# One ScalarE pass of an add-and-GELU kernel, moved ahead of three copies

## The chip, the cores and the metric

The kernel runs on one core of a Trainium2 chip. The metric is the device time of one execution in microseconds (us). A core has several engines that run their own instruction streams side by side and wait for each other through semaphores: VectorE (DVE in the profile), ScalarE (ACT), GpSimd (POOL), SyncE (SP), which here only issues DMA transfers, and TensorE (PE), which this kernel does not use. Sixteen DMA engines move data between the chip's main memory (DRAM, or HBM in the profile) and the core's own memories.

## The reference

Two float32 matrices of 1024 x 4096 are added, and the tanh form of GELU is applied to each element:

```
def reference(x, y):
    z = x + y
    return (0.5 * z * (1 + np.tanh(np.sqrt(2 / np.pi) * (z + 0.044715 * z ** 3)))).astype(np.float32)
```

Each matrix has 16.78 MB; two are read and one is written, 50.33 MB in all.

## The kernel before

The 1024 rows are spread over 128 partitions, eight rows to each, so that a partition holds 32,768 elements. The kernel treats them as one line cut in two halves of 16,384. Tile `z` (line by line: x, then x + y, then the result) holds the whole line. Tile `y` holds only half a line, so y's second half can be loaded only when all adds of the first half have read y's first half. Tile `ps` is a buffer in PSUM, a second memory of the core, for copies of some of x's chunks.

Transfers are all issued by SP, in this order: y's first 704 columns and the rest of y's first half, x's first half, x's second half (four loads that wait for nothing), y's second half (waits for the adds of chunks 0 to 8), the first store (waits for the gelus of chunks 0 to 8), the second store (waits for the gelus of chunks 9 to 19). One function issues each kind: `load_x` (L130), `load_y` (L135), `store` (L139).

The work on the line is cut in 20 chunks. Chunks 0 and 1 have 1024 columns and chunks 2 to 8 have 2048; these are the first half. Chunk 9 has 512 columns, 10 has 1536, 11 to 16 have 2048, 17 has 1024, 18 and 19 have 512; these are the second half. For a chunk there are up to three steps:

- `copy(c)` (L143), on ScalarE, only for chunks 2 to 6 and 9 to 11: x's chunk is copied from `z` to `ps`.
- `add(c)` (L150): on VectorE, or for chunks 7, 8 and 12 on GpSimd. It reads x's chunk (from `ps` if there is a copy, else from `z`) and y's chunk, and writes the sum to `z`.
- `gelu(c)` (L162), on ScalarE: GELU of the chunk, in place in `z`.

The order on each engine is written out by hand in lists: `on_vector`, `on_gpsimd`, and for ScalarE `on_scalar` (L98), a list of steps and chunks. A loop at the end of the kernel takes the steps from these lists in turn and emits each once the steps that it needs have been emitted; the order within a list is never changed. ScalarE therefore does, in this order: copies 2 to 6, gelus 0 and 1, copies 9 to 11, gelus 2 to 19. Copies 9 to 11 need x's second half; gelu 2 needs only the add of chunk 2.

Two functions edit the finished program: one moves the first two loads ahead of the start-up barrier, the other lets the wait for the last store happen later. They are not touched.

Of the kernel before, what the change touches and what calls it, by code (L numbers as in the profile page):

```python
# [66 lines left out]
def kernel(  # L67
# [27 lines left out]
    copies = {2: 0, 3: 2048, 4: 0, 5: 2048, 6: 0, 9: 0, 10: 512, 11: 2048}  # L95
    on_vector = [0, 1, 2, 3, 4, 5, 6, 9, 10, 11, 13, 14, 15, 16, 17, 18, 19]
    on_gpsimd = [7, 8, 12]
    on_scalar = [("copy", c) for c in (2, 3, 4, 5, 6)] + [("gelu", 0), ("gelu", 1)] + [("copy", c) for c in (9, 10, 11)] + [("gelu", c) for c in range(2, 20)]  # L98
    held = {7: 1}

    def ranges(sizes):
# [137 lines left out]
```

## Time and profile before

| what | value |
|---|---|
| time, median of 3 runs (lowest to highest) | 120.17 us (120.0 to 120.55) |
| time of the profiled execution | 120.21 us |
| its span (first to last instruction or transfer in the profile) | 118.7 us |
| data moved, mean rate over the span | 50.33 MB, 424 GB/s |
| ScalarE busy | 44.1 us (37%), 30 instructions |
| VectorE busy | 29.1 us (25%), 18 instructions |
| GpSimd busy | 13.7 us (12%), 7 instructions |
| a gelu of 128 x 2048 | 1.90 us, 13 of them |
| a copy of 128 x 2048 | 1.87 us, 6 of them |
| an add of 128 x 2048 on VectorE / on GpSimd | 2.28 us / 4.53 us |

How the views are read: the order of time has, in each line, the start in us, the length, the engine, the line of the kernel (L162 is line 162), the operation, what it writes and reads (`z<-ps,y` writes z from ps and y), the shapes, how many instructions were merged (`x7`), and in brackets how long the engine had been idle before and what ended that. `SPq` is SP issuing a transfer; where two issues are merged (`x2`), the length reaches from the first to the end of the second. The chain that ended last is followed back from the end of the program, at each step to what released it. The view by stretches has, for each stretch of time, its length, the busy time of VectorE, ScalarE and GpSimd with the number of their instructions, the clock of TensorE (1.00 here, without meaning), the DMA engines' share and the GB/s moved. In this view a DMA packet is booked whole in the stretch in which it starts, so in a short stretch the share can exceed 1.

### The profile page before, as it was taken

The page shows a single profiled execution, that of the slowest core. Times are in us where ns is not written, and L with a number is a line of the kernel's source. Part 1 is how long each engine was busy: PE and PEld are TensorE (multiplying, and loading weights), DVE is VectorE, ACT ScalarE, POOL GpSimd, SP SyncE. Part 2 cuts the span into 40 slices and gives each one's busy share as a digit, 9 for nine tenths or more (in the row PEclk, how much of TensorE's full clock was granted, in tenths as well). Part 3 has the DMA queues.
Part 4 walks back from the last instruction along what each step waited for, and adds up shares of the span by engine and source line. Part 5 has one row for each costly group of instructions (what it writes and reads, how often), then busy time and mean ns, then how long its engine had stood idle before and what let it go on. Part 6 is the DMA issues. An engine that isn't in the chain of part 4 may idle for free.

```text
span 118.7 us, 115 instructions
## 1 busy us (share of the span) xinstructions
DVE 29.1 (25%) x18; ACT 44.1 (37%) x30; POOL 13.7 (12%) x7
## 2 busy tenths in 40 slices
DVE  0000000000000299992000000009999920000000
ACT  5000000000000296890069999804799980000000
POOL 0000000000000039960000000009500000000000
DMA  9779978988899889988898889988899888988891
GB/s 460 338 338 613 402 338 360 685 353 353 353 640 420 353 353 464 596 353 353 353 707 353 353 353 530 530 353 353 353 618 442 353 353 353 707 353 353 353 662 44
DMA packets 1008, 50.33 MB, mean 424 GB/s; under 512 B 112, under 2 KB 112, under 8 KB 240
## 3 DMA queue, kind: packets, MB, share of 16 engines
q1 hardware_dynamic: 1008, 50.33, 98.6%
HBM read 33.55 MB, written 16.78 MB: 424 GB/s over the span
## 4 chain that ended last, share of the span: by engine, by line
DMA 55%; DVE 14%; ACT 10%; DVEq 1%; ACTq 0%; issue 0%; SPq 0%
DMA z<-in_x_dram 33%; DMA y<-in_y_dram 22%; DVE z L150 14%; ACT z L162 10%; DVEq L206 1%; ACTq L206 0%; DVEq L150 0%; SPq L135 0%
## 5 line engine op out<-in xcount | busy, mean ns | idle before, releaser
L162 ACT ACTIVATE z<-z 128x2048 f32<-128x2048 f32 (+3 forms) x20 | 29.7, 1556 | 5.9 <-DVE z L150 5.9
L143 ACT COPY ps<-z 128x2048 f32<-128x2048 f32 (+2 forms) x8 | 13.0, 1654 | 46.3 <-DMA z<-in_x_dram 44.6
L150 DVE TENSOR_TENSOR z<-z,y 128x2048 f32<-128x2048 f32 (+2 forms) x9 | 13.6, 1573 | 39.5 <-DMA z<-in_x_dram 39.5
L150 DVE TENSOR_TENSOR z<-ps,y 128x2048 f32<-128x2048 f32 (+2 forms) x8 | 15.6, 2015 | 25.9 <-DMA y<-in_y_dram 25.9
L150 POOL TENSOR_TENSOR z<-z,y 128x2048 f32<-128x2048 f32 x3 | 13.5, 4526 | 70.7 <-DVE z L150 42.9
L191 ACT ACT_TABLE_LOAD x1 | 1.3, 1283 | 1.3 <-PEq L223 1.3
L190 DVE MEMSET one<- 128x1 f32 x1 | 0.1, 59 | 1.3 <-PEq L223 1.3
L191 ACT ACTIVATE one<-one 128x1 f32<-128x1 f32 x1 | 0.2, 202 | 0.0
L223 POOL MEMSET const-float32-0.0<- 128x1 f32 x1 | 0.1, 98 | 0.2 <-issue 0.2
L223 POOL MEMSET const-uint8-127<- 128x1 uint8 x1 | 0.1, 102 | 0.0
L223 POOL MEMSET const-bfloat16-1.0<- 128x1 bf16 x1 | 0.1, 101 | 0.0
L223 POOL MEMSET const-float32-1.0<- 128x1 f32 x1 | 0.1, 98 | 0.0
## 6 DMA issues: line engine op xcount, KB each, us to landing
y<-in_y_dram SPq DMA_DIRECT2D x1, 7840.0 KB, 21.0
y<-in_y_dram SPq DMA_DIRECT2D x1, 352.0 KB, 3.0
z<-in_x_dram SPq DMA_DIRECT2D x2, 49.0
out_dram<-z SPq DMA_DIRECT2D x2, 21.9
y<-in_y_dram SPq DMA_DIRECT2D x1, 25.7
```

Source lines behind the costliest of these rows:

```text
L143: nc.scalar.copy(out=in_psum(c), in_=zt[:, a:b])
L150: ins = eng.tensor_add(out=zt[:, a:b], in0=first, in1=yt[:, o : o + b - a])
L162: nc.scalar.activation(out=zt[:, a:b], in_=zt[:, a:b], func=act.Gelu_apprx_tanh)
L190: nc.vector.memset(one[:, :1], 0.0)
L191: nc.scalar.activation(out=one[:, :1], in_=one[:, :1], func=act.Gelu_apprx_tanh)
L206: tc.compile()
L223: nc = _bacc.Bacc("TRN2", target_bir_lowering=False, num_devices=1)
```

## The change

One list is edited. In ScalarE's order the gelu of chunk 2 stands behind gelu 1 and ahead of copies 9, 10 and 11; before, it stood behind these copies. No step is added or left out, and no size, buffer, engine or transfer changes.

```
-    on_scalar = [("copy", c) for c in (2, 3, 4, 5, 6)] + [("gelu", 0), ("gelu", 1)] + [("copy", c) for c in (9, 10, 11)] + [("gelu", c) for c in range(2, 20)]
+    on_scalar = [("copy", c) for c in (2, 3, 4, 5, 6)] + [("gelu", 0), ("gelu", 1), ("gelu", 2)] + [("copy", c) for c in (9, 10, 11)] + [("gelu", c) for c in range(3, 20)]
```

In the built program ScalarE's list differs in this alone: one gelu of 128 x 2048 stands ahead of the three copies, and six instead of seven stand behind them. The lists of VectorE, GpSimd and SP, and what each of their instructions waits for, are the same in both.

## The prediction

> **What bounds the kernel now.** I read the page first, for the share of the DMA engines, then the order of time, then the chain that ended last, and at last the DMA traffic in stretches of one microsecond.
>
> ```profile
> span 118.7 us, 115 instructions
> ...
> q1 hardware_dynamic: 1008, 50.33, 98.6%
> ```
>
> The one DMA queue keeps the 16 DMA engines at work for 98.6% of the span; ACT, the busiest compute engine, has 37%. So an ACT pass matters only through the moment at which it lets a transfer start. The order of time shows these moments:
>
> ```profile
> 51.72 2.00 ACT L162 ACTIVATE z<-z 128x1024 f32<-128x1024 f32 x2
> 54.35 0.33 SPq L135 DMA_DIRECT2D y<-in_y_dram  x1
> 60.28 3.76 ACT L143 COPY ps<-z 128x512 f32<-128x512 f32 x3 [6.56 <-DMA z<-in_x_dram]
> 63.98 12.70 ACT L162 ACTIVATE z<-z 128x2048 f32<-128x2048 f32 x7
> 76.70 21.29 SPq L139 DMA_DIRECT2D out_dram<-z  x2
> 80.14 4.55 DVE L150 TENSOR_TENSOR z<-ps,y 128x512 f32<-128x512 f32 x3 [25.86 <-DMA y<-in_y_dram]
> ...
> 84.72 12.89 ACT L162 ACTIVATE z<-z 128x2048 f32<-128x2048 f32 x9 [0.71 <-DVE z L150]
> ```
>
> ACT ends gelu 1 at 53.72 and stands still for 6.56 us until x's second half lands. Then come copies 9 to 11 and seven gelus (chunks 2 to 8), and at 76.70 SP issues the first store. But the second half of y, issued at 54.35, is still under way then: DVE gets it at 80.14. The issue of the first store is therefore not on the chain that ended last, which goes from y's second half straight to the second half's work:
>
> ```profile
> 54.35 25.67 DMA y<-in_y_dram
> ...
> 80.14 0.69 DVE z L150
> ...
> 84.72 11.86 ACT z L162 x7
> ...
> 97.10 0.52 ACT z L162
> ```
>
> The last view counts DMA packets by their start, in stretches of 1 us. A transfer of half a tensor is eight rounds of 16 packets of 64 KB, one per engine; a row with 1049 GB/s holds exactly one round (16 x 65,536 B in 1 us), and its DMA share (next to last column) is then the mean time of a packet in us.
>
> ```profile
> 54.50:55.50 1.00, 0.00 (x0) 0.00 (x0) 0.00 (x0) 1.00 2.43 1049
> 56.90:57.90 1.00, 0.00 (x0) 0.00 (x0) 0.00 (x0) 1.00 2.42 1049
> 59.30:60.30 1.00, 0.00 (x0) 0.02 (x1) 0.00 (x0) 1.00 2.43 1049
> 73.70:74.70 1.00, 0.00 (x0) 1.00 (x1) 0.00 (x0) 1.00 2.42 1049
> 76.10:77.10 1.00, 0.00 (x0) 0.57 (x1) 0.00 (x0) 1.00 2.66 1049
> 78.90:79.90 1.00, 0.00 (x0) 0.00 (x0) 0.00 (x0) 1.00 2.43 1049
> 95.80:96.80 1.00, 0.03 (x1) 1.00 (x2) 0.00 (x0) 1.00 2.42 1049
> 98.40:99.40 1.00, 0.00 (x0) 0.00 (x0) 0.00 (x0) 1.00 2.44 1049
> ```
>
> The rounds follow each other at the length of a packet, also from one transfer to the next: x's last round starts in 56.9 to 57.9 and y's first in 59.3 to 60.3. The reader is to see two things. First, y's last round (76.1 to 77.1) is followed by the first store's first round (78.9 to 79.9) with no hole: the store was there in time. Second, that last round alone took 2.66 us a packet, not 2.42. The store was issued in the midst of it (76.70).
>
> **The change, part by part.** *Moved out of the late run:* one gelu of 128x2048. Seven of them take 12.70 us, so one is 12.70 / 7 = 1.81 us (the mean of one, 1.90 us, overlaps its neighbour). Gelus 3 to 8 then run from 63.98 to 74.89, and the first store is issued at about 74.9 instead of 76.70.
>
> *Moved into the idle time:* gelu 2 runs from 53.72 to about 55.6. It issues no DMA. Its add ran third on DVE (two adds of 1024, then chunk 2, from 40.92 on) and ended near 45.5, so it waits for nothing. The copies behind it wait for x's second half until 60.28 as before: cost 0, hidden by 6.56 - 1.9 = 4.7 us of idle ACT; without that idle time it would be 1.81 us. On DVE 0.55 us of add 6 lie beside it (to 54.28); a lengthening there would delay the issue of y's second half, whose first packets start only after 59.3, so some 5 us cover that. DVE, GpSimd and SP keep their order and their waits. SP's queue has only the first store and, behind it, the second store, which waits for the last gelu (97.6) in both kernels.
>
> *The store's earlier issue.* The second store shows the lead that an issue needs: issued at 97.64, its first packets start in the row 98.40 to 99.40, so at most 1.76 us. The first store has 78.9 - 76.70 = 2.2 us at least. It was in time already, so 1.8 us more of lead fill no hole: 0 us from the wait itself. The queue has served transfers in the order of issue (y's first half, x's two halves and y's second half landed one after another), so y's second half should land at 80.0 as before, the second half's chain end at 97.6 and the span stay at 118.7.
>
> *The one price that the trace does not show* is what becomes of the slow last round. On the mean it loses 2.66 - 2.42 = 0.24 us. On the path it loses more: x's first half landed at 1.26 + 39.53 = 40.79, its second at about 1.6 + 58.6 = 60.2 (DMA issue to landing, longest), y's second half at 54.35 + 25.67 = 80.02; the steps are 19.4 and 19.8 us, so about 0.4 us. Three rows bound it. If it belongs to the change from loading to storing, it stays: 0. If it comes from the store's packets reaching the queue while the last load packets are in flight, an issue before that round starts (74.9, the round starts after 76.1) should cost what y's second half cost when it was issued at 54.35, ahead of x's last round: 2.43 and 2.42 us, that is 0.01; the gain is up to 0.4 us. If it grows with the time for which both are in the queue, it gets worse by 0.4 us (worked out below). I take 0: the round is the only one in which a load is followed by a store, and issues behind a load (54.35) and behind a store (97.64) cost 0.01 to 0.02 us a packet, so direction is the one thing that sets it apart beyond doubt.
>
> *Sum.* The profiled execution took 120.21 us, 118.7 of it span and 1.5 around it; it stands 0.04 above the median of 120.17. 120.21 + 0 (gelu 2 early) + 0 (store's wait) + 0 (slow round) = 120.2 us.
>
> **The rivals.**
>
> *A: the slow round goes.* The nearest row in position (issue one round ahead, 0.01 us) speaks for it, the different direction against it. Y's second half lands 0.4 us earlier, DVE and ACT follow, the second store is issued at 97.2 instead of 97.64, and the first store, whose packets are shifted by as much, ends in time for it. 120.21 - 0.4 = 119.8 us; with the slowest engine losing more than I read from the landings, down to 119.6.
>
> *B: the early store disturbs the load for longer.* Place: the last rounds of y's second half. An issue takes effect about 0.9 us later (97.64 to the first packets of the second store, taken as 98.5), so the store is in the queue from 77.6; y's last packets end about 79.7. That is 2.1 us for a loss of 0.4. Issued at 74.9 it would be there from 75.8, 3.9 us: 0.4 x 3.9 / 2.1 = 0.74, so 0.34 more. It passes to the end in full, because the second store has no slack: the first store's last round starts in 95.8 to 96.8 and ends 2.42 later, 98.2 to 99.2, just where the second store's packets begin. 120.21 + 0.34 = 120.55 us, slower than before. It decides from the moment at which the next to last round of y shows over 2.5 us a packet. Against it: the round of 73.70 and all before it are at 2.42 whatever ACT does, and an issue cost a load 0.01 where the next transfer was a load.
> The Trainium skill, "DMA: Bandwidth & Descriptors", section "Two DMAs through the same engine are not ordered", says that descriptors on one queue of an engine start in order but are pipelined, with reading and writing as separate queues. By that rule the store could begin to read while the load's last packets are still being written, which would speak for B; the trace shows a slow round there, but not what slows it.
>
> *C: load and store packets take turns.* If the store's packets, queued earlier, went ahead of y's last round, y would land a packet, 2.42 us, later, the last gelu would end at 100.0 and the second store start 2.42 us late: 120.21 + 2.4 = 122.6 us. Against it: no store packet started before y's last round in the trace, and queued transfers have landed in order.
>
> *D: the change does not do what it says*, because ACT's copies or the store wait for something else. The store would be issued at 76.7 again: 120.2 us. The listing of each engine's instructions speaks against it, the idle 6.56 us too; the time is the same as in the forecast.
>
> **How the numbers follow.** Forecast 0.53, A 0.30, B 0.10, C 0.03, D 0.02, something unseen 0.02. A measurement of this kernel tells about 0.5% (0.6 us) from no change: 119.57 and 120.77 are the bounds. A reaches past the lower one only if the slowest engine's loss is well above 0.4 us, a third of its chance: 0.10, and 0.02 for the unseen and the scatter of runs (120.0 to 120.55) on the forecast: faster 0.12. Slower: C 0.03, a third of B 0.03, scatter and unseen 0.03: 0.09. The rest, 0.79, is within 0.5%. The range reaches down to A's lowest, 119.6, and up past B to 120.7.
>
> **What would show it.** Gelu 2 at 53.7 and the copies still at 60.3; the first store issued at 74.9; its first packets still in 78.9 to 79.9, without a hole; DVE's first add of the second half at 80.1; the second store issued at 97.6. The row 76.10 to 77.10 decides between forecast (2.66), A (2.42) and B (over 2.66, and the row before it raised too). Store packets that start before 78 would be C. The prediction is wrong if y's second half lands more than 0.6 us earlier or later than 80.0, or if a hole opens between the two stores.

## The result and the profile after

The changed kernel is slower: 121.08 us in the median of 6 runs (120.82 to 121.48) against 120.19 for the kernel before (120.0 to 120.55), a ratio of 1.0081 with a 95% interval of 1.0064 to 1.0098. Its profiled execution took 120.98 us with a span of 119.5 us; before, these were 120.21 and 118.7.

The order of time, with the lines that answer to those shown of the kernel before:

```profile
51.75 3.80 ACT L162 ACTIVATE z<-z 128x1024 f32<-128x1024 f32 x3
54.38 0.33 SPq L135 DMA_DIRECT2D y<-in_y_dram  x1
60.32 3.76 ACT L143 COPY ps<-z 128x512 f32<-128x512 f32 x3 [4.77 <-DMA z<-in_x_dram]
64.02 10.90 ACT L162 ACTIVATE z<-z 128x2048 f32<-128x2048 f32 x6
74.94 23.86 SPq L139 DMA_DIRECT2D out_dram<-z  x2
80.95 4.55 DVE L150 TENSOR_TENSOR z<-ps,y 128x512 f32<-128x512 f32 x3 [26.64 <-DMA y<-in_y_dram]
...
85.54 12.89 ACT L162 ACTIVATE z<-z 128x2048 f32<-128x2048 f32 x9 [0.71 <-DVE z L150]
```

On ScalarE the change did what it says. Gelu 2 joined gelus 0 and 1 (x3, to 55.55), the copies began with x's second half as before, and the first store was issued at 74.94 instead of 76.70. But VectorE got y's second half at 80.95, not at 80.14. Everything behind it is late by the same 0.8 us: ScalarE's last run starts at 85.54 instead of 84.72. The chain that ended last names the piece that grew:

```profile
54.38 26.45 DMA y<-in_y_dram
...
80.95 0.69 DVE z L150
...
97.92 0.52 ACT z L162
```

y's second half took 26.45 us from issue to landing, 0.78 more than before (25.67). That is the whole growth of the span (119.5 - 118.7 = 0.8). The DMA packets by their start show where in that transfer it lies; as before, a row with 1049 GB/s holds one round of 16 packets of 64 KB, and its share is the mean time of a packet in us:

```profile
71.30:72.30 1.00, 0.00 (x0) 1.00 (x2) 0.00 (x0) 1.00 2.42 1049
73.70:74.70 1.00, 0.00 (x0) 1.00 (x1) 0.00 (x0) 1.00 2.43 1049
76.10:77.10 1.00, 0.00 (x0) 0.00 (x0) 0.00 (x0) 1.00 3.60 1049
79.70:80.70 1.00, 0.00 (x0) 0.00 (x0) 0.00 (x0) 1.00 2.43 1049
```

y's last round took 3.60 us a packet, where it had taken 2.66. The rounds before it, and the store's first round behind it (79.7 to 80.7), are at the usual 2.42 to 2.43. Issued 1.76 us earlier, the store did not start earlier: its first packets began at 79.9 us, where they had begun at 79.0. What changed is the one round ahead of it.

### The profile page after: what moved, and what is told of

Read it like the earlier page. It is cut to its first block, busy times and chain, and to the rows that moved or that the text cites. A ratio compares the mean times of both kernels' runs of the same rounds, so it can differ in the third digit from the quotient of the medians.

```text
span 119.5 us, 115 instructions
## 1 busy us (share of the span) xinstructions
DVE 29.1 (24%) x18; ACT 44.1 (37%) x30; POOL 13.8 (12%) x7
## 4 chain that ended last, share of the span: by engine, by line
DMA 55%; DVE 14%; ACT 10%; DVEq 1%; ACTq 0%; issue 0%; SPq 0%
DMA z<-in_x_dram 33%; DMA y<-in_y_dram 22%; DVE z L150 14%; ACT z L162 10%; DVEq L206 1%; ACTq L206 0%; DVEq L150 0%; SPq L135 0%
```

## The experiments

Theory 1: a store that stands in the queue behind y's second half slows y's last round. The first rivals are that gelu 2's new place costs the time in some other way, that every turn from load to store has a fixed price, and that the loss grows with the time in the queue (B of the prediction). The first four runs move the store's issue; later ones ask what of the store it is. For each, the loss is the share of y's last round less that of the round before it. It is read from two rows, 73.70 to 74.70 and 76.20 to 77.20 unless others are shown: in the kernel before 2.66 - 2.42 = 0.24 us, in the changed one 3.60 - 2.43 = 1.17. Each loss comes from one execution, and the rounds ahead of the last one lie between 2.42 and 2.48 us in these rows, so 0.05 us of a loss mean nothing.

Where the issue of the store is moved, a line from the order of time stands first: the store's issue, merged with that of the second store (x2).

**after_held: gelu 2 early, store late**

On the changed kernel, the end of ScalarE's list and the new step:

```
-[("gelu", c) for c in range(3, 20)]
+[("gelu", c) for c in range(3, 8)] + [("idle", 0), ("idle", 1)] + [("gelu", c) for c in range(8, 20)]
...
+    def idle(i):
+        a = 1024 * i
+        nc.scalar.activation(out=one[:, :992], in_=zt[:, a : a + 992], func=act.Gelu_apprx_tanh)
```

> Gelu 2 stays ahead of the copies, but ScalarE makes two more passes of 992 columns (of finished results, into a tile that nothing reads) ahead of gelu 8, so that the first store is issued near 76.8 us, where it was before the change, not at 74.9. Theory 1 (the early store in the queue slows y's last round): the round in 76.1 to 77.1 falls back from 3.60 to about 2.65 us a packet, and the time to 120.2 us. Rival (something else about gelu 2's new place costs the time, its pass in the idle stretch or the order of the copies): the time stays at 121.1 us.

```profile
77.06 20.85 SPq L139 DMA_DIRECT2D out_dram<-z  x2
...
73.70:74.70 1.00, 0.00 (x0) 0.97 (x2) 0.00 (x0) 1.00 2.46 1049
76.20:77.20 1.00, 0.00 (x0) 0.83 (x1) 0.00 (x0) 1.00 2.43 1049
```

With the store issued at 77.06, the loss was gone (2.43 after 2.46) and the time fell to 119.94 us, a ratio to the kernel before of 0.9992 (0.9971 to 1.0013). Gelu 2's new place by itself costs nothing that this interval shows: the first rival falls. The round came out faster than the 2.65 expected; the next run bears on that.

**g1_early: the store one more pass later than in the kernel before**

ScalarE's list behind copies 2 to 6, against the kernel before (for the next two runs as well):

```
-[("gelu", 0), ("gelu", 1)] + [("copy", c) for c in (9, 10, 11)] + [("gelu", c) for c in range(2, 20)]
+[("gelu", 0)] + [("copy", c) for c in (9, 10, 11)] + [("gelu", c) for c in range(1, 20)]
```

> Gelu 1 goes behind the copies too, so that the first store is issued about 0.95 us later than in the kernel before, at 77.65 us, and its packets can reach the queue from about 78.5 (second store before: 97.64 to 98.50). Theory 1: the last round of y is by then nearly done and takes 2.42 to 2.50 us a packet, y's second half lands at 79.6, no hole opens ahead of the store, and the time is 119.6 to 119.9 us. Rival (the slow round is the price of turning from loads to stores, whenever the store is issued): the round stays at 2.66 and the time at 120.2 us or a little above.

```profile
77.76 19.89 SPq L139 DMA_DIRECT2D out_dram<-z  x2
...
73.70:74.70 1.00, 0.00 (x0) 1.00 (x2) 0.00 (x0) 1.00 2.45 1049
76.20:77.20 1.00, 0.00 (x0) 1.00 (x1) 0.00 (x0) 1.00 2.44 1049
```

The store was issued at 77.76 and the loss was gone here too (2.44 after 2.45); the next packets followed without a hole. The time was 119.85 us, ratio 0.999 (0.9973 to 1.0006): in the expected direction, but not clear of 1. The same kernel was therefore run again, as **g1_again**:

> The same kernel as g1_early, for a narrower interval. Theory 1: 0.25 us of the slow round saved, 119.85 to 119.95 us, ratio 0.998. Rival: no difference, 1.000.

```profile
73.70:74.70 1.00, 0.00 (x0) 1.00 (x2) 0.00 (x0) 1.00 2.42 1049
76.20:77.20 1.00, 0.00 (x0) 1.00 (x1) 0.00 (x0) 1.00 2.43 1049
```

119.8 us against 120.16, ratio 0.9974 (0.9956 to 0.9992): this time clear of 1, by 0.26%, and the lowest median of all runs. The two series put the gain at 0.10% and 0.26%. In this chain y's second half took 25.20 us, 0.47 less than before. In both executions the turn from load to store cost nothing: it has no fixed price.

**g0_early: later still**

```
+[("copy", c) for c in (9, 10, 11)] + [("gelu", c) for c in range(0, 20)]
```

> Gelus 0 and 1 both go behind the copies: the first store is issued about 78.6 us, its packets can start from about 79.45. Theory 1: y's last round takes 2.42, y's second half lands at 79.6, but the engines stand still from about 79.0 until 79.45; the second store is then not waited for, and the span is about that of g1_early plus 0.3 us: 119.9 to 120.2 us. Rival (a price of turning): 2.66 and a hole of some tenths of a us on top: 120.6 us.

```profile
78.80 19.35 SPq L139 DMA_DIRECT2D out_dram<-z  x2
...
74.20:75.20 1.00, 0.00 (x0) 1.00 (x2) 0.00 (x0) 1.00 2.42 1049
76.70:77.70 1.00, 0.00 (x0) 1.00 (x2) 0.00 (x0) 1.00 2.42 1049
79.30:80.30 1.00, 0.01 (x1) 0.00 (x0) 0.00 (x0) 1.00 2.45 1049
```

The store was issued at 78.80. The last round is clean, but the store's first packets began 0.17 us after the first engine was free (79.65 against 79.48 in the trace). The time was 120.27 us, ratio 1.0023 (1.0008 to 1.0037), a little above the expected span. The hole is not all of it. In this execution seven of y's earlier rounds, from 55 to 72 us, took 2.47 to 2.52 us (2.42 to 2.43 in g1_again), so y's last packets ended at 79.48 to 79.81, over 0.5 us later than in g1_again, and the engine that was free last had no hole. Why these rounds were slow is not known. Without them the store, with its first packets at 79.65, would have been late on every engine (g1_again's ended their load at 78.83 to 79.29). So an issue at 78.80 is too late; of the moments tried, 77.06 and 77.75 cost nothing.

**g5_early: much earlier**

```
+[("gelu", c) for c in range(0, 5)] + [("copy", c) for c in (9, 10, 11)] + [("gelu", c) for c in range(5, 20)]
```

> Gelus 2, 3 and 4 all go into the idle stretch: the first store is issued about 71.3 us, two rounds of y ahead of its last one instead of just ahead of it. Theory 1 with a limit (only the last load packet can be slowed, by a store that is queued behind it): the last round takes 3.6 us as in the changed kernel, the rounds before it 2.42 to 2.43, and the time is 121.1 us as there. Rival B as it was predicted (the loss grows with the time for which both are in the queue): another 3.6 us in the queue, several rounds slow, 122 us or more.

```profile
71.49 27.39 SPq L139 DMA_DIRECT2D out_dram<-z  x2
...
73.70:74.70 1.00, 0.00 (x0) 0.00 (x0) 0.00 (x0) 1.00 2.46 1049
76.20:77.20 1.00, 0.00 (x0) 0.00 (x0) 0.00 (x0) 1.00 3.48 1049
```

Issued at 71.49, 3.45 us ahead of the changed kernel, the store cost no more: 3.48 - 2.46 = 1.02 us, and 121.08 us, the same median as the changed kernel (ratio to before 1.0088, 1.0069 to 1.0108). The loss has a limit and does not grow with the time in the queue. (The round ahead, 2.46, is above the 2.43 expected, but after_held shows the same 2.46 with no store in the queue.)

**s992 and s256: how many bytes stand behind the load.** Both are built on g1_early, whose last round is clean; the first new line is that of s992, the second that of s256.

```
-    stores = [16384, 16384]
+    stores = [992, 15392, 16384]
+    stores = [256, 16128, 16384]
```

> Built on g1_early. The first store is cut in two: 992 columns (31.7 KB per DMA engine, eight packets of 4 KB) are stored from 54.8 us on, queued right behind y's second half, the other 15,392 columns when gelu 8 is done, at 77.7. Theory H1 (behind the last load packet the engine already reads ahead for the store, and loses the time of what it reads, up to some 30 KB: 1.1 us at the 27 GB/s at which a 64 KB packet takes 2.42 us): y's last round takes about 3.4 us a packet, for 31.7 KB / 27.1 GB/s = 1.17 at most. Theory H2 (a price of about 1 us for each turn from load to store, whatever the store's size): 3.5 us as well. This run is the anchor for s256.

> As s992 with 256 columns (8.2 KB per engine, eight packets of 1 KB) in the early piece. H1: only 8.2 KB can be read ahead, 0.30 us, so y's last round takes about 2.7 us a packet. H2: about 3.5 us, as with the large store.

s992, then s256:

```profile
73.70:74.70 1.00, 0.00 (x0) 1.00 (x2) 0.00 (x0) 1.00 2.43 1049
76.20:77.20 1.00, 0.00 (x0) 1.00 (x1) 0.00 (x0) 1.00 3.63 1049
```

```profile
73.70:74.70 1.00, 0.00 (x0) 1.00 (x2) 0.00 (x0) 1.00 2.46 1049
76.20:77.20 1.00, 0.00 (x0) 1.00 (x1) 0.00 (x0) 1.00 2.76 1049
```

An engine moves 65,536 B in 2.42 us, 27.1 KB per us. s992 lost 3.63 - 2.43 = 1.20 us, worth 32.5 KB, with 31.7 KB queued; s256 lost 0.30 us, worth 8.1 KB, with 8.2 KB queued. The loss is the time of the queued store's own bytes. With a whole store queued (512 KB per engine) y's round lost 1.17 and 1.02 us, worth 28 to 32 KB: a limit near there. The fixed price (H2) falls. ScalarE was busy in the row of y's last round in s992 as in g1_again (1.00), so it is not ScalarE's standing still there (0.00 in the changed kernel) that slows the round. (Single runs took 121.21 and 120.30 us, beside one of 119.89 for the kernel before, whose runs reach from 119.75 to 120.76; only the first is clear of them.)

**ss992 and dd992: which end of the store it is**

On g1_early, queued behind y's second half, first ss992, then dd992:

```
+        nc.sync.dma_start(out=one[:, :992], in_=zt[:, :992])
+        nc.sync.dma_start(out=spare[:, :], in_=xv[:, :992])
```

> Built on g1_early. Queued behind y's second half is no store but a transfer of 992 columns from z to the unused tile, both in SBUF, which the output does not need; the first store comes whole at 77.7. If reading from SBUF beside the load's writing into SBUF is what costs, y's last round takes about 3.4 us as in s992; if it is the writing to DRAM, 2.45.

> Built on g1_early. Queued behind y's second half is a transfer of 992 columns of x from DRAM to a spare tensor in DRAM, which the output does not need; the first store comes whole at 77.7. If reading from SBUF is what costs (or reading ahead from a faster source), y's last round takes 2.42 to 2.45 us; if writing to DRAM or any change of direction costs, about 3.4 as in s992.

ss992, then dd992:

```profile
73.70:74.70 1.00, 0.00 (x0) 1.00 (x2) 0.00 (x0) 1.00 2.45 1049
76.20:77.20 1.00, 0.00 (x0) 1.00 (x1) 0.00 (x0) 1.00 3.19 1049
```

```profile
73.70:74.70 1.00, 0.00 (x0) 1.00 (x2) 0.00 (x0) 1.00 2.42 1049
76.20:77.20 1.00, 0.00 (x0) 1.00 (x1) 0.00 (x0) 1.00 2.43 1049
```

The same bytes read from DRAM and written to DRAM cost y's round nothing (2.43 after 2.42). Read from SBUF and written to SBUF, they cost 0.74 us. So a loss needs a transfer that reads SBUF; writing to DRAM by itself costs nothing. ss992 lost less than the 1.2 us of s992, and what is queued behind the load differs only in where it writes; whether writing to DRAM adds to the loss is open. (These two kernels and the next three move more bytes than the others, so their times, 122.06, 121.22, 121.16, 134.58 and 122.12 us in this order, are not compared.)

**s_half and ss_tail: within an engine, or at SBUF**

On g1_early, first s_half, queued behind y's second half (spare is 64 x 1024), then ss_tail, queued behind the second store:

```
+        nc.sync.dma_start(out=spare[:, :], in_=zt[:64, :1024])
+        nc.sync.dma_start(out=yt[:, :8192], in_=zt[:, :8192])
```

> Built on g1_early. Queued behind y's second half is a transfer of 64 partitions x 1024 columns from z to a spare tensor in DRAM, which the output does not need: four packets of 4 KB, 16.4 KB, for each of the 16 engines, read from partitions 0 to 63 alone; the first store comes whole at 77.7. If the loss arises within an engine (its own read-ahead), all 16 packets of y's last round are lengthened alike, by about 16.4 KB / 27.1 GB/s = 0.6 us. If it arises where SBUF is read and written at once, only the engines that are writing partitions 0 to 63 lose, about 1.2 us each, and the others nothing: two groups of 8, near 3.6 and 2.45 us.

> Built on g1_early. Behind the second store the kernel also moves 8192 finished columns from z to y's tile, both in SBUF (eight packets of 32 KB per engine), which the output does not need; the time is longer by that. If SBUF cannot be read and written by the same engine at full rate, these packets take about 2.4 us each (half rate) and the time is about 139 us; if the two directions are independent, 1.2 us each and 129.5 us.

s_half:

```profile
73.70:74.70 1.00, 0.00 (x0) 1.00 (x2) 0.00 (x0) 1.00 2.48 1049
76.20:77.20 1.00, 0.00 (x0) 1.00 (x1) 0.00 (x0) 1.00 3.01 1049
```

The loss is 0.53 us, near the 0.6 of 16.4 KB per engine, and the 16 packets of that round lie between 2.96 and 3.10 us in the trace: one group, not two. Each engine lost about the time of its own share of the bytes.
The Trainium skill, "DMA: Bandwidth & Descriptors", section "The descriptor swizzle", gives engines 0 to 7 the partitions 0 to 63 in such a load; that the engines split this way is taken from there, no run here shows it. By that split the loss does not follow the partitions that are read.
A limit that all engines share would give one group too. Against it speaks the kernel before, where some packets of y's last round took 2.43 us and others up to 2.97: the engines were not hit alike.

ss_tail, the second store's last round and two rounds of the move within SBUF (32 KB packets, so a whole round shows 524 GB/s):

```profile
115.00:116.00 1.00, 0.00 (x0) 0.00 (x0) 0.00 (x0) 1.00 2.42 1049
117.40:118.40 1.00, 0.00 (x0) 0.00 (x0) 0.00 (x0) 1.00 1.64 524
119.20:120.20 1.00, 0.00 (x0) 0.00 (x0) 0.00 (x0) 1.00 1.83 524
```

The first round took 1.64 us, later ones 1.83. 1.83 us for 32,768 B is 17.9 KB per us, two thirds of the rate of a load or a store. Neither expectation holds: an engine that reads and writes SBUF is slower, but not by half. If that lower rate were all that lies behind the loss, 8.2 KB read at 17.9 KB per us would take 0.46 us, in which a load writes 8.2 KB instead of 12.4, a loss of 0.15 us; s256 lost 0.30, the full time of the bytes. The rows show something else as well: the move was queued behind the second store from 97.89 us on, and that store's last round kept its 2.42. A transfer that reads SBUF slowed a load ahead of it, but not a store.

**ld992_after: another load between**

On the changed kernel, queued between y's second half and the first store:

```
+        nc.sync.dma_start(out=one[:, :992], in_=xv[:, :992])
```

> Built on the changed kernel (store issued at 74.9). Between y's second half and the first store a load of 992 columns of x into the unused tile is queued (31.7 KB per engine), which the output does not need. H1 (the loss hits whatever is the last load ahead of the store): y's last round goes back to 2.42 to 2.5 us, y's second half lands at 79.6, and the small load takes the loss instead: its eight packets of 4 KB together about 1.2 + 1.1 us. Rival (the loss hits y's transfer itself, through its wait or its tile): y's last round stays at 3.6.

```profile
73.70:74.70 1.00, 0.00 (x0) 1.00 (x1) 0.00 (x0) 1.00 2.43 1049
76.20:77.20 1.00, 0.00 (x0) 0.00 (x0) 0.00 (x0) 1.00 2.91 1049
```

Half a hit for H1. y's last round lost 0.48 us, not 1.17, and the eight small packets of each engine, 0.154 us each in s992, took 0.218 in the mean (both from the traces): another 8 x 0.064 = 0.51 us. (Against the packets of dd992, which like these are read from DRAM and took 0.175, it is 0.35 us.) Together that is 0.8 to 1.0 us, nearly the same loss, spread over the last load bytes ahead of the store, whichever transfer they belong to. That y's round still lost something would mean, if the store is read ahead, that this began while more than the 31.7 KB of the small load was still to be written.

## Why the prediction was wrong

It forecast 120.2 us, within 119.6 to 120.7; the kernel took 121.08.

- *Gelu 2 in the idle stretch, cost 0*: right. It ended at 55.55, the copies began at 60.32 with x's second half, and after_held, with gelu 2 early, is no slower than the kernel before.
- *First store issued at 74.9, nothing gained by the wait*: right (74.94). No hole had to be filled.
- *The price of the slow round, taken as 0*: the step that failed. It argued that direction was the one thing that set that round apart "beyond doubt", and so put the 0.24 us down to the turn from load to store, at whatever moment the store is issued. g1_early and g0_early make the same turn without loss. What the runs showed in its place: a store that stands in the queue behind the load costs the load's last bytes the time of some 30 KB of the store, and whether it does depends on when it is issued. In the kernel before, issued when y's last round was already under way, it cost 0.24 us; 1.8 us sooner it cost the full 1.17. The difference, 0.93 us in the mean over the engines, came out as 0.78 us on y's landing and 0.9 us in the medians.
- *Rival A, the slow round goes*: took the issue of y's second half behind x's as the nearest row. That row has a load behind a load; dd992 shows that bytes read from DRAM cost nothing there, so it could not stand for a store.
- *Rival B* had the place, the sign and the way to the end right: the round ahead of the store, and a second store without slack. Its size was wrong: 0.34 us from growth in proportion to the time in the queue. g5_early refutes the proportion, and its sign of a raised round ahead of the last one did not show (2.43). The bound from above should not have been a line through one point that lay at the edge: in the trace of the kernel before, the packets of that round lie between 2.43 and 2.97 us, some engines hardly touched, so the full cost was not to be read there. Its input was off too: the slowest packet lost 2.97 - 2.42 = 0.55 us, not the 0.4 taken from the landings. And "the round of 73.70 and all before it are at 2.42" is not exact, since y's first half moved at 2.31 to 2.39 us in smaller packets; nothing rests on that.
- The rule of the Trainium skill that was weighed there ("DMA: Bandwidth & Descriptors", "Two DMAs through the same engine are not ordered": started in order but pipelined, with reading and writing as separate queues) fits what the runs show: the store's packets start behind the load's, and yet 8.2 KB of them queued cost the load 0.30 us. As quoted it gives no size.
- *Rival C, packets taking turns*: no; the store's packets began at 79.94, on each engine right behind y's last packet.
- *Slack of the second store, none*: right. The late landing of y went to the end in full (VectorE 0.81 us late, ScalarE's last gelu at 97.92 instead of 97.10).

Left open: how the queued store takes time from the load, and why only if it reads SBUF. That an engine reads some 30 KB ahead of its writing, and that bytes from SBUF then take the place of load bytes still on their way from DRAM, would fit s992, s256, s_half and dd992, but it is a guess: no run shows the reading itself. The exact edge is open too: in the kernel before and in after_held the store was issued at about the same point of y's last round (76.70 in a round that starts from 76.42; 77.06 in one that starts from 76.76), and the loss was 0.24 and none. Only one execution of the kernel before was traced, of 120.21 us; its other runs reach from 119.75 to 120.76, so the 0.24 may differ from run to run.

## What to carry to other kernels

A store that becomes ready while the last load is still being moved was best issued just before that load ended. An issue 1.1 to 1.5 us before the ends of the load's packets (77.75 us, with ends from 78.83 to 79.29 in the trace of g1_again) left no hole and cost nothing. Issued 2.8 us sooner, in the changed kernel, it made y's load 26.45 us long instead of 25.20, and since computation waited for that load, the delay came out at the end (121.08 against 119.80 us). Before a wait on a saturated queue is shortened, ask not only whether the transfer has a hole to fill, but what the engines do with it while the one ahead is still under way.

## What the runs showed of the hardware

- A transfer that reads SBUF, queued behind a load from DRAM, slows the load's last packets by about the time of its own bytes, up to a limit near 28 to 32 KB per engine: 0.30 us for 8.2 KB, 0.53 for 16.4, 1.20 for 31.7, 1.02 and 1.17 for a whole store. Written to SBUF instead of DRAM, 31.7 KB cost 0.74 us. A transfer from DRAM to DRAM cost 0.01, a store that was issued in time (77.75) the same. A store ahead of a transfer that reads SBUF was not slowed (2.42 in ss_tail). That the engine reads ahead would fit this; it was not seen directly.
- A move of 4 MB within SBUF ran at 17.9 KB per us and engine (286 GB/s over the 16), against 27.1 for a load or a store. This is not a rate for every such move: the 4 KB packets of ss992 took 0.154 us, 25.8 KB per us, right after y's slowed round.
- The order of transfers in the queue is kept (store packets at 79.94 in the changed kernel, right behind y's on each engine), yet a transfer can delay the one ahead of it.
